# Attention outputs in a PSUM bank of the projections instead of one of the scores: a two-layer decoder trunk on one core

## The chip, the cores and the metric

The kernel runs on one core of a Trainium2 chip. The metric is the device time of one execution in microseconds (us). The engines are TensorE (PE in the profile, with PEld for its weight loads), VectorE (DVE), ScalarE (ACT), GpSimd (POOL) and SyncE (SP), which issues the DMAs. TensorE writes its results to PSUM, which this kernel uses as eight banks of 128 x 512 f32; the other engines read them from there.

## What is computed

```python
h = x
for l in range(2):
    h = h + hybrid_mixer(rmsnorm(h, attn_norm[l]), ...)
    h = h + memory_cross_attention(rmsnorm(h, cross_norm[l]), rmsnorm(mem, mem_norm[l]), ...)
    h = h + squared_relu_mlp(rmsnorm(h, mlp_norm[l]), w1[l], w2[l])
return rmsnorm(h, final_norm)
```

`h` is 512 tokens by 1024. The mixer has 16 causal attention heads with values 64 wide: six MLA heads, six differential heads (two softmaxes each, subtracted) and four MoBA heads. Their outputs are concatenated and go through one 1024 x 1024 output projection. Cross attention has four heads over 256 memory tokens. All is f32.

## The kernel before

Activations lie transposed, features on partitions and the 512 tokens on the free axis. An f32 product is made of three matmuls (`mm3`): each operand is held as a high part and a rest, and the product of the two rests is left out. A projection of 128 features is so 8 blocks x 3 = 24 matmuls 128 x 512, all in one PSUM bank (`proj_steps`, and `proj` for a whole one at once).

PSUM is shared out by tags. `psum(tag)` (L130 to L132) hands out a bank of its tag, `self.pbufs` says how many banks a tag has ("mm" 3, "s" 3, "t" 2), and `self.ptags` says which tag stands for another. Within a tag the banks are given out in the order of the program: a new tile takes the bank that comes free first, and its first matmul waits until that bank was read. What takes them:

- "mm": projections, and a few other products of the fillers.
- "s": the scores of one block of 128 queries (`scores`, L633). VectorE's pass L638 reads a score with its bias, and with that its bank is free; ScalarE's exponential (L640) works on a copy in SBUF.
- "o": the attention output of one head (`mix`, L668 to L680): eight matmuls of values with probabilities. ScalarE copies one half (L679) and VectorE adds the other half to it (L680); then the bank is free. The cross attention's outputs (`tail` in `cross_units`) take "o" too. Before, "o" stands for "s".
- "t": transposes of probabilities (L280), 128 x 128 each, which ScalarE (L660) and VectorE (L663) read.

In a mixer the 16 heads are run in eight pairs. A head is four units, one for each block of queries, with scores 128, 256, 384 and 512 wide: `start` makes scores, exponential and the division by their sum (L699 and L700; L700 of the 256-wide ones on GpSimd), `finish` makes the transposes, and after the fourth the head's `mix` follows. `pipeline` writes these one behind the other with a skew of two units between a start and its finish, and two more before the mix, and puts pieces of coming projections between them (`Filler`). When all heads are started the fillers are used up; `output` then writes the eight output projections, each over the heads' pairs in the order 3, 0, 4, 1, 5, 2, 6, 7, and their sums go to `h` in L1080.

The matmuls of `mm3` and of `scores` are not held to the order of the program: a scheduler of the compiler's places them where their inputs and their bank are there. So the first output projections can stand between the last attention steps, as far as they have a bank.

Of the kernel before, what the change touches and what calls it, by code (L numbers as in the profile page):

```python
# [49 lines left out]
class Filler:  # L50
# [17 lines left out]
    def run(self, time):  # L68

        busy = False  # L70
        while self.todo and self.todo[0][2] in self.over and time > 0:
            time -= self.step()
            busy = True
        return busy
# [27 lines left out]
class Trunk:  # L102
# [1313 lines left out]
    def run(self):  # L1416
        nc = self.nc
        self.bufs = {"A": 8, "B": 21, "tmp": 11, "small": 40, "raw": 4, "w": 5, "pt": 2}
        self.pbufs = {"mm": 3, "s": 3, "t": 2}
        self.ptags = {"o": "s"}  # L1420

        self.fill_order = "kv cq tok m0 d0 m1 d1 o0 m2 d2 o1 mem cross"
        self.unit_order = "m0 d0 m1 d1 o0 m2 d2 o1"
        self.fill_time = {1: 1870, 2: 1700}
        self.cross_fill_time = 4000
        self.mem_time = 300

        self.skew, self.tail_skew = 2, 2

        self.wait_n, self.wait_l, self.wait_d = 8, 3, 3  # L1430
        self.pow_d = 3
        self.chain_n, self.chain_l, self.chain_d, self.chain_k = 6, 12, 4, 2

        self.pool_kinds = ("mq", "kr", "q", "cq", "lat")
        self.vector_full = self.vector_all = False

        self.look, self.mlp_look = 2, 6
        self.plan = self.planned()
        self.blocks = sum(1 for _ in self.planned())
        self.fetched = 2  # L1440
        self.setup()
        g = self.gains
        self.sum_squares_start()
        self.hn = [self.norm_input(k, g["g_attn"][:, :KT], squares=False) for k in range(KT)]
        for k in range(KT):
            self.after(2 + k, lambda k=k: self.sum_squares_add(self.h[k], True))
        self.hnorm = Later()
        self.after(10, lambda: self.norm_of(self.hnorm, self.sq, NQ, 2))
        self.setup_gains()
        self.after(12, self.setup_rotary)  # L1450
        for n, part in enumerate(self.setup_distances()):
            self.after(24 + 2 * n, part)
        self.after(58, self.setup_lambda)
        self.memory_norm(34, 8)
        for l in range(L):
            gs = slice(l * KT, (l + 1) * KT)
            self.vector_full = True
            outs = self.mixer(l)
            self.vector_full = False
            self.output(self.a["w_out"][l], outs, g["g_cross"][:, gs], (3, 0, 4, 1, 5, 2, 6, 7))  # L1460
            outs = self.cross(l)
            parts = {n: [] for n in ("11", "21", "22", "t1", "t2", "t3", "t4", "y")}
            self.vector_all = True
            self.output(self.a["w_co"][l], outs, g["g_mlp"][:, gs], halves=parts)
            self.mlp(l, g["g_attn"][:, (l + 1) * KT:(l + 2) * KT] if l + 1 < L else None, parts)
            self.vector_all, self.look = False, 2
# [101 lines left out]
```

## Time and profile before

| | us |
|---|---|
| three runs | 1529.02, 1529.40, 1532.49 |
| median | 1529.40 |
| profiled execution, its own time | 1527.16 |
| its span in the trace | 1525.3 |

The profiled execution is the one that all rows below come from; its mean granted TensorE clock was 0.994. A span is the time from the first to the last instruction that the trace shows; the 1.86 us to the execution's own time lie around it. In a timeline a row gives the start of a group of like instructions, how long the group took, the engine, the line of the kernel, the operation, the tile that it writes and those it reads, shapes, the number of instructions, and in brackets the idle time of the engine just before it with what ended it.

### The profile page before, as it was taken

The page shows a single profiled execution, that of the slowest core. Times are in us where ns is not written, and L with a number is a line of the kernel's source. Part 1 is how long each engine was busy: PE and PEld are TensorE (multiplying, and loading weights), DVE is VectorE, ACT ScalarE, POOL GpSimd, SP SyncE. Part 2 cuts the span into 40 slices and gives each one's busy share as a digit, 9 for nine tenths or more (in the row PEclk, how much of TensorE's full clock was granted, in tenths as well). Part 3 has the DMA queues.
Part 4 walks back from the last instruction along what each step waited for, and adds up shares of the span by engine and source line. Part 5 has one row for each costly group of instructions (what it writes and reads, how often), then busy time and mean ns, then how long its engine had stood idle before and what let it go on. Part 6 is the DMA issues. An engine that isn't in the chain of part 4 may idle for free.

```text
span 1525.3 us, 24601 instructions
## 1 busy us (share of the span) xinstructions
PE 1481.2 (97%) x8648; PEld 1295.4 (85%) x8648; DVE 1060.3 (70%) x2422; ACT 856.9 (56%) x1887; POOL 365.3 (24%) x302
## 2 busy tenths in 40 slices
PE   7899999999999999999999999999999999999997
PEld 6778897888899899998897888878888989899887
DVE  7688888536699666675537898873378976677753
ACT  5666777535566544454446677764366654445441
POOL 2645375442000000000145446644400000000001
PEclk9999999999999999999999999999999999999998
DMA  4434543231223323322224535423212332333331
GB/s 153 127 106 138 153 132 111 77 96 49 87 74 125 111 88 105 100 96 98 96 77 112 150 113 154 118 86 95 98 34 76 106 123 90 104 96 106 111 97 55
DMA packets 90139, 157.24 MB, mean 103 GB/s; under 512 B 12065, under 2 KB 17057, under 8 KB 90017
## 3 DMA queue, kind: packets, MB, share of 16 engines
q1 hardware_dynamic: 89728, 155.63, 33.2%
q8 instruction: 68, 1.11, 0.3%
q14 instruction: 55, 0.44, 0.1%
q10 hardware_dynamic: 288, 0.05, 0.0%
HBM read 136.24 MB, written 2.10 MB: 91 GB/s over the span
## 4 chain that ended last, share of the span: by engine, by line
PE 71%; DVE 10%; issue 9%; ACT 4%; DMA 3%; POOL 2%; SPq 0%; POOLq 0%; DVEq 0%; ACTq 0%
PE mm L277 58%; PE s L277 10%; PE t L280 2%; DMA raw<-w 2%; DVE tmp L638 1%; ACT tmp L640 1%; DVE tmp L703 1%; POOL w L162 1%; DVE pt L663 1%; ACT B L140 1%; DMA raw<-w_in 1%; DVE small L1001 1%; POOL B L142 1%; PE t L277 1%; DVE tmp L261 1%
## 5 line engine op out<-in xcount | busy, mean ns | idle before, releaser
L277 PE MATMUL mm<-B,w 128*128 128x512 f32 (+1 forms) x2490 | 574.4, 386 | 1.3 <-POOL B L142 1.3
L277 PEld LDWEIGHTS mm<-B,w 128*128 128x128 f32 x2490 | 453.0, 189 | 95.1 <-POOL B L142 2.6
L277 PE MATMUL mm<-A,w 128*128 128x512 f32 (+1 forms) x1920 | 386.7, 351 | 6.2 <-ACT A L144 5.8
L157 ACT CAST w<-raw 128x512 fp32r<-128x512 f32 (+1 forms) x372 | 225.1, 607 | 269.6 <-PE mm L277 208.0
L277 PEld LDWEIGHTS mm<-A,w 128*128 128x128 f32 x1920 | 311.8, 190 | 50.7 <-ACT A L144 5.8
L162 POOL TENSOR_TENSOR w<-raw,w 128x512 fp32r<-128x512 f32 (+2 forms) x180 | 228.0, 1273 | 220.1 <-ACT w L157 177.9
L410 POOL TENSOR_TENSOR tmp<-tmp,tmp 128x512 f32<-128x512 f32 (+1 forms) x25 | 30.8, 1234 | 655.7 <-ACT tmp L407 653.6
L162 DVE TENSOR_TENSOR w<-raw,w 128x512 fp32r<-128x512 f32 x192 | 134.4, 700 | 35.5 <-ACT w L157 35.2
L640 ACT ACTIVATE tmp<-tmp,small 128x384 f32<-128x384 f32 (+3 forms) x176 | 99.0, 562 | 66.0 <-DVE small L638 63.2
L1080 DVE TENSOR_TENSOR h<-mm,h 128x512 f32<-128x512 f32 x92 | 63.3, 688 | 70.9 <-PE mm L277 70.6
L140 ACT CAST B<-tmp 128x512 fp32r<-128x512 f32 (+2 forms) x156 | 91.9, 591 | 24.1 <-DVE tmp L680 4.8
L277 PE MATMUL mm<-pt,B 128*128 128x256 f32 x768 | 102.9, 283 | 2.4 <-ACT tmp L1319 2.4
L277 PEld LDWEIGHTS mm<-pt,B 128*128 128x128 f32 x768 | 95.8, 189 | 3.4 <-ACT tmp L1319 3.4
L261 DVE TENSOR_TENSOR tmp<-raw,raw 128x512 f32<-128x512 f32 x64 | 44.0, 688 | 65.9 <-DMA raw<-w 65.9
L264 ACT CAST B<-tmp 128x512 fp32r<-128x512 f32 x96 | 59.5, 620 | 50.8 <-DVE tmp L261 50.8
L142 DVE TENSOR_TENSOR B<-tmp,B 128x512 fp32r<-128x512 f32 (+1 forms) x110 | 75.5, 686 | 12.3 <-ACT B L140 8.3
L280 PE MATMUL t<-ident,tmp 128*128 128x128 f32 (+1 forms) x444 | 74.5, 274 | 9.3 <-DVE tmp L828 3.3
L280 PEld LDWEIGHTS t<-ident,tmp 128*128 128x128 f32 (+1 forms) x444 | 54.2, 140 | 24.8 <-issue 4.2
L142 POOL TENSOR_TENSOR B<-tmp,B 128x512 fp32r<-128x512 f32 (+1 forms) x46 | 61.4, 1340 | 49.7 <-ACT B L140 47.4
L663 DVE TENSOR_TENSOR pt<-t,pt 128x256 fp32r<-128x256 f32 (+1 forms) x192 | 67.1, 370 | 6.3 <-ACT pt L660 5.4
L277 PE MATMUL s<-pt,B 128*128 128x512 f32 (+3 forms) x352 | 71.0, 345 | 0.0
L339 POOL TENSOR_TENSOR small<-small,mhalf 128x4 f32<-128x4 f32 (+2 forms) x19 | 23.4, 1229 | 198.2 <-DVE small L373 174.5
(195 smaller groups left out, 2135.8 us busy)
## 6 DMA issues: line engine op xcount, KB each, us to landing
raw<-w SPq DMA_DIRECT2D x256, 256.0 KB, 2.9
raw<-w_in SPq DMA_DIRECT2D x64, 256.0 KB, 3.0
st<-B SPq DMA_DIRECT2D x144, 64.0 KB, 2.0
raw<-w_ck SPq DMA_DIRECT2D x32, 256.0 KB, 2.9
raw<-w_cv SPq DMA_DIRECT2D x32, 256.0 KB, 2.7
raw<-w_out SPq DMA_DIRECT2D x32, 256.0 KB, 2.7
raw<-w_cq SPq DMA_DIRECT2D x32, 256.0 KB, 2.7
raw<-w_co SPq DMA_DIRECT2D x32, 256.0 KB, 2.6
```

Source lines behind the costliest of these rows:

```text
L140: nc.scalar.copy(hi, x)
L142: eng.tensor_tensor(lo, x, hi.bitcast(F32), ALU.subtract)
L157: self.nc.scalar.copy(w[:, 0, :], raw)
L162: eng.tensor_tensor(w[:, 1, :], raw, w[:, 0, :].bitcast(F32), ALU.subtract)
L261: nc.vector.tensor_tensor(got[name], x, y, op)
L264: nc.scalar.copy(w[:, 0, :], raw)
L277: self.in_order(self.nc.tensor.matmul(out, lhs, rhs, start=start, stop=stop, skip_group_check=open), hold)
L280: self.in_order(self.nc.tensor.transpose(out, x, self.ident))
L410: eng.tensor_tensor(s[:, :n], s[:, :n], self.sq[:, :n], ALU.add)
L640: nc.scalar.activation(t[:, :n], t[:, :n], AF.Exp, bias=st[:, 0:1], scale=-1.0, accum_out=st[:, 1:2])
L663: nc.vector.tensor_tensor(lo, src, hi.bitcast(F32), ALU.subtract)
L1080: nc.vector.tensor_tensor(self.h[m], ps, self.h[m], ALU.add)
```

## The change

One entry of a table: "o" stands for "mm". An attention output, in the mixers and in cross attention, takes one of the three banks of the projections, and the scores have their three banks with the few other tiles of "s" alone. The number of banks and all instructions stay as they are.

```diff
--- before.py
+++ after.py
@@ -1417,7 +1417,7 @@
         nc = self.nc
         self.bufs = {"A": 8, "B": 21, "tmp": 11, "small": 40, "raw": 4, "w": 5, "pt": 2}
         self.pbufs = {"mm": 3, "s": 3, "t": 2}
-        self.ptags = {"o": "s"}
+        self.ptags = {"o": "mm"}
 
         self.fill_order = "kv cq tok m0 d0 m1 d1 o0 m2 d2 o1 mem cross"
         self.unit_order = "m0 d0 m1 d1 o0 m2 d2 o1"
```

What this does to the order of instructions is seen in three places.

The first is TensorE's order near the end of layer 0's mixer. `s_` are the scores of the last head, `t_` transposes, `mm_3659`, `mm_3700` and `mm_3742` the first three output projections; `s_3599` is the output of the last head but one, `mm_3599` after the change. Before, and then after:

```order
L280 MATMUL t_3547<-ident,tmp_3473 128x128 x4
L277 MATMUL mm_3659<-B_1806,w_3459 128x512 x3
L277 MATMUL s_3556<-st_2331,st_2252 128x384
L277 MATMUL s_3556<-st_2332,st_2252 128x384
L277 MATMUL mm_3659<-B_1278,w_3459 128x512
L277 MATMUL s_3583<-st_2331,st_2252 128x512
L277 MATMUL s_3583<-st_2332,st_2252 128x512
L277 MATMUL t_3566<-halves,tmp_3511 128x2 x4
L277 MATMUL mm_3659<-B_1278,w_3459 128x512 x2
L277 MATMUL mm_3659<-B_2542,w_3485 128x512 x3
L277 MATMUL mm_3659<-B_2028,w_3459 128x512
L280 MATMUL t_3579<-ident,tmp_3516 128x128
```

```order
L280 MATMUL t_3547<-ident,tmp_3473 128x128 x4
L277 MATMUL s_3556<-st_2331,st_2252 128x384
L277 MATMUL s_3556<-st_2332,st_2252 128x384
L277 MATMUL s_3583<-st_2331,st_2252 128x512
L277 MATMUL s_3583<-st_2332,st_2252 128x512
L277 MATMUL t_3566<-halves,tmp_3511 128x2 x4
L280 MATMUL t_3579<-ident,tmp_3516 128x128
L280 MATMUL t_3593<-ident,tmp_3540 128x128 x2
L277 MATMUL mm_3599<-pt_3465,B_2550 128x512 x2
```

Between these transposes and scores stood ten matmuls of the projection `mm_3659` ahead of `t_3579`; now none does, and the last two scores stand one behind the other.

The second is the very end of the same mixer, with the last head's output (`s_3644`, then `mm_3644`). Before, and then after:

```order
L280 MATMUL t_3626<-ident,tmp_3586 128x128 x4
L277 MATMUL mm_3700<-B_2028,w_3662 128x512 x2
L277 MATMUL mm_3742<-B_1806,w_3703 128x512 x2
L280 MATMUL t_3635<-ident,tmp_3616 128x128 x4
L277 MATMUL s_3644<-pt_3578,B_2550 128x512 x2
L277 MATMUL s_3644<-pt_3578,B_2550 128x384 x2
L277 MATMUL s_3644<-pt_3578,B_2550 128x256 x2
L277 MATMUL s_3644<-pt_3578,B_2550 128x128 x2
L277 MATMUL mm_3742<-B_1806,w_3703 128x512
L277 MATMUL mm_3659<-B_3641,w_3485 128x512
```

```order
L280 MATMUL t_3626<-ident,tmp_3586 128x128 x4
L280 MATMUL t_3635<-ident,tmp_3616 128x128 x4
L277 MATMUL mm_3644<-pt_3578,B_2550 128x512
L277 MATMUL mm_3659<-B_1806,w_3459 128x512
L277 MATMUL mm_3644<-pt_3578,B_2550 128x512
L277 MATMUL mm_3644<-pt_3578,B_2550 128x384 x2
L277 MATMUL mm_3644<-pt_3578,B_2550 128x256 x2
L277 MATMUL mm_3644<-pt_3578,B_2550 128x128 x2
L277 MATMUL mm_3659<-B_1806,w_3459 128x512 x2
L277 MATMUL mm_3659<-B_1278,w_3459 128x512 x3
```

Before, 26 matmuls of output projections stand ahead of the last matmul of `s_3644`, from `mm_3659` to the third one's beginning. After, one matmul of `mm_3659` stands there, and the other 25 come behind. Layer 1 shows the same.

The third is the beginning of a differential pair in the middle of the mixer, with the waits that TensorE's instructions carry in brackets. The head's output `s_1826` (`mm_1826` after the change) stands right ahead of it. Before, and then after:

```order
L277 MATMUL s_1838<-st_1309,st_1194 128x128 [waits DMAHW5_49,DMAHW7_49,DMAHW3_49,DMAHW1_49]
L277 MATMUL s_1844<-st_1309,st_1194 128x128 [waits DMAHW4_49,DMAHW2_49,DMAHW6_49,DMAHW0_49,DVE_49]
L277 MATMUL mm_1769<-A_138,w_1652 128x512 x3
L277 MATMUL mm_1769<-A_141,w_1652 128x512 x3
L277 MATMUL mm_1769<-A_144,w_1652 128x512 x3
L280 MATMUL t_1865<-ident,tmp_1754 128x128 [waits DVE_49]
L280 MATMUL t_1865<-ident,tmp_1754 128x128 x2
L277 MATMUL s_1873<-st_1309,st_1194 128x256 [waits DVE_49]
L277 MATMUL s_1879<-st_1309,st_1194 128x256 [waits DVE_49]
L277 MATMUL mm_1897<-A_123,w_1772 128x512 x3
```

```order
L277 MATMUL s_1838<-st_1309,st_1194 128x128 [waits DMAHW5_49,DMAHW7_49,DMAHW3_49,DMAHW1_49]
L277 MATMUL s_1844<-st_1309,st_1194 128x128 [waits DMAHW4_49,DMAHW6_49,DMAHW2_49,DMAHW0_49]
L277 MATMUL mm_1769<-A_138,w_1652 128x512 x3
L277 MATMUL mm_1769<-A_141,w_1652 128x512 x3
L277 MATMUL mm_1769<-A_144,w_1652 128x512 x3
L280 MATMUL t_1865<-ident,tmp_1754 128x128 [waits DVE_49]
L280 MATMUL t_1865<-ident,tmp_1754 128x128 x2
L277 MATMUL s_1873<-st_1309,st_1194 128x256
L277 MATMUL s_1879<-st_1309,st_1194 128x256 [waits DVE_49]
L277 MATMUL mm_1897<-A_123,w_1772 128x512 x3
```

The second 128-wide score and the first 256-wide one lose their wait for VectorE; the second 256-wide one keeps it.

## Rows read from the trace of the kernel before

**Rows 1.** The page's head: span, busy time and number of instructions by engine.

```profile
span 1525.3 us, 24601 instructions
...
PE 1481.2 (97%) x8648; PEld 1295.4 (85%) x8648; DVE 1060.3 (70%) x2422; ACT 856.9 (56%) x1887; POOL 365.3 (24%) x302
```

**Rows 2.** PE's list of waits: waiting group, releaser: us in all, times, longest.

```profile
PE s L277 <- DVE small L638: 4.1, 6, 1.2
PE s L277 <- DVE tmp L680: 3.4, 7, 0.7
```

**Rows 3.** Timeline of PE at three scores that wait in layer 0's mixer.

```profile
100.52 0.33 PE L277 MATMUL s<-st,st 96*128 96x128 f32 x1 [1.09 <-DVE small L638]
...
109.05 0.51 PE L277 MATMUL s<-st,st 96*128 96x512 f32 x1 [0.19 <-DVE small L638]
...
144.51 0.59 PE L277 MATMUL s<-st,st 96*128 96x256 f32 x2 [0.47 <-DVE tmp L680]
```

**Rows 4.** Timeline of DVE around the last of them.

```profile
143.79 0.67 DVE L680 TENSOR_TENSOR tmp<-s,tmp 64x512 f32<-64x512 f32 x1
144.39 0.27 DVE L638 CUSTOM_DVE_ANT_0 tmp<-s,dneg 128x128 f32<-128x128 f32 x1
```

**Rows 5.** Timeline of PE at the end of both mixers, layer 0 first.

```profile
263.00 0.61 PE L277 MATMUL s<-st,st 128*128 128x384 f32 x2 [0.63 <-DVE tmp L680]
...
266.54 1.18 PE L277 MATMUL mm<-B,w 128*128 128x512 f32 x4
267.61 0.41 PE L280 MATMUL t<-ident,tmp 128*128 128x128 f32 x2
...
269.37 2.09 PE L277 MATMUL mm<-B,w 128*128 128x512 f32 x8
271.47 0.63 PE L280 MATMUL t<-ident,tmp 128*128 128x128 f32 x4
...
272.86 0.60 PE L280 MATMUL t<-ident,tmp 128*128 128x128 f32 x4
273.21 1.48 PE L277 MATMUL s<-pt,B 128*128 128x512 f32 x8
274.53 38.56 PE L277 MATMUL mm<-B,w 128*128 128x512 f32 x166
...
1007.91 0.62 PE L277 MATMUL s<-st,st 128*128 128x384 f32 x2 [0.62 <-DVE tmp L680]
...
1019.45 38.56 PE L277 MATMUL mm<-B,w 128*128 128x512 f32 x166
```

**Rows 6.** Timeline of DVE and PE at a projection's bank.

```profile
127.42 0.69 DVE L960 TENSOR_TENSOR tmp<-mm,rows 128x512 f32<-128x512 f32 x1
...
130.09 1.07 PE L277 MATMUL mm<-B,w 128*128 128x512 f32 x4
```

**Rows 7.** Timeline of POOL and DVE at the end of layer 0's mixer.

```profile
265.59 0.93 POOL L700 TENSOR_SCALAR tmp<-tmp,small 128x256 f32<-128x256 f32 x1 [6.57 <-DVE small L699]
...
268.88 0.68 DVE L638 CUSTOM_DVE_ANT_0 tmp<-s,dneg 128x512 f32<-128x512 f32 x1
...
270.84 0.48 DVE L700 TENSOR_SCALAR tmp<-tmp,small 128x512 f32<-128x512 f32 x1
```

**Rows 8.** Two gaps of PE; stretches: us, busy us by engine, granted clock, DMA.

```profile
76.40 0.63 PE L280 MATMUL t<-ident,tmp 128*128 128x128 f32 x4 [2.38 <-DVE tmp L700]
...
246.09 0.73 PE L277 MATMUL mm<-w,A 128*128 128x512 f32 x2 [1.11 <-DVE B L145]
...
76.00:80.00 4.00, 3.60 (x13) 3.15 (x14) 3.83 (x13) 2.52 (x8) 1.01 (x1) 0.64 0.29 69
80.00:84.00 4.00, 4.00 (x18) 3.20 (x18) 2.63 (x9) 2.06 (x6) 1.30 (x2) 0.94 0.38 87
244.00:248.00 4.00, 2.89 (x14) 2.05 (x13) 3.58 (x11) 2.39 (x7) 1.82 (x2) 1.00 0.38 92
```

## The prediction

> **What bounds the kernel now.** I read the page's head first: TensorE (PE) is busy 97% of the 1525.3 us span, VectorE (DVE) 70%, ScalarE (ACT) 56% [rows 1]. The time is therefore PE's work plus the few places where PE stands still, and the change can act in two ways only: it takes PE waits away or makes new ones, and it changes what PE has to fill a wait with. So I read PE's list of waits next. Scores wait for VectorE's L638 (the pass that frees a score's bank) six times, 4.1 us together, and for L680 (the add that frees the bank of an attention output) seven times, 3.4 us [rows 2]: at most 7.5 us, 0.5% of the span. Then I read the timeline at those waits, to see what would be late next, and the order of instructions against the changed one, to see what moves. The largest move is at the end of each mixer, so the rest of my reading is the timeline of that stretch, 263 to 274.5 us in layer 0. Layer 1 repeats it: from its wait of 0.62 us at 1007.91 to the start of the long run of projections at 1019.45 are 11.54 us, against 11.53 in layer 0 [rows 5].
>
> **Bulk: the score waits.** With "o" out of the scores' banks, scores alone rotate over the three. In the order a score loses its wait for VectorE and the next one keeps it. The trace says what that is worth. At 144.51 a score stood 0.47 us for L680 [rows 3]. L680 ran from 143.79 for 0.67 us, and right behind it, from 144.39 for 0.27 us, stands the L638 that frees the next bank [rows 4]. Without L680 the first score of the pair goes some 0.45 us earlier, but the second needs the bank of that L638, which ends at 144.66, while it now starts about 0.3 us behind the first, at 144.8. The gain is 0.1 us. The other kind, 1.09 us at 100.52, ends earlier too, but a 512-wide score at 109.05 already waits 0.19 us for L638 [rows 3]: what PE gains it gives back there, since VectorE is no faster. I take 0.1 us for each of six or so such places: **-0.6 us**. The bounds are 0 and the whole of what stands in rows 2 less the 0.63 and 0.62 us of the two mixer ends [rows 5], 7.5 - 1.25 = 6.2 us.
>
> The Trainium skill, in "Perfetto Trace Analysis", section "Optimization Strategy", says that the same gap repeating on the engine that should be saturated can mean that there isn't enough PSUM for the next tile to be allocated. By that page the whole 6.2 us would come back here; it is a rival below. The trace agrees that a bank is waited for, and does not agree that a bank is all that is missing.
>
> **Bulk: the projections.** An "o" now takes one of the projections' three banks, and the order shows new waits at the start of some projections. One is the projection at 130.09, which takes the bank that L960 reads from 127.42 for 0.69 us [rows 6]: it is free 1.98 us before it is wanted. I cost these waits at nothing. What covers them is those 2 us; if VectorE were later by more, each would cost the difference.
>
> **The mixer's end.** In the order before, 26 matmuls of the first three output projections stand between the last attention steps of a layer; they fill PE while VectorE and ScalarE finish the softmax. A projection there needs a bank of "mm". After the change the last two outputs stand ahead of the projections in that pool, and of the 26 only one stands before the last output's end; 25 come behind it. One dense matmul costs 38.56 / 166 = 0.232 us [rows 5], so **25 x 0.232 = 5.8 us** of PE work goes from inside the waits to behind them.
>
> Against that the chain of the last attention steps, now alone on PE, gets shorter. By rows: the 384-wide score goes at 261.43 or so instead of 263.00, since its wait of 0.63 us was for L680 [rows 5]; that is worth little, as VectorE reads the scores one after another. The first transposes were ready before PE had time for them: POOL's L700 ended at 265.59 + 0.93 = 266.52 [rows 7], and its transposes began at 267.61 behind projections [rows 5]. So they begin at 266.6, a gain of 1.0 us. From there the chain belongs to VectorE and ScalarE: the 512-wide L638 began at 268.88 behind short passes, its L700 at 270.84 [rows 7], and the four transposes at 271.47 [rows 5], 0.15 us after L700's end at 271.32. Moving each step up as far as its inputs allow, I get transposes at 271.1, the next four at 272.05 (were 272.86), the last output from 272.4 (was 273.21). The chain shortens by **0.8 us**. So the long run of projections, which began at 274.53, begins at 273.7 and has 25 matmuls more: 5.8 - 0.8 = **+5.0 us a layer, +10.0 us** for two. Bounds: +5.8 a layer if the chain does not shorten at all; and 0 if every step up to the last output moves up by as much as the fillers took from it (a rival).
>
> **The clock.** After the change PE stands idle about 1.5, 1.4, 2.5 and 0.4 us within 8 us there; the long one lies between the transposes of the 384-wide and those of the 512-wide score. What a gap does to PE's clock I take from the rows nearest in length. After 2.38 us at 76.40 the granted clock was 0.64 of 2.4 GHz in 76 to 80 us and 0.94 in 80 to 84; after 1.11 us at 246.09 it stayed 1.00 [rows 8]. 0.64 is a mean of the two levels, 1.2 and 2.4 GHz. The loss is (0.36 + 0.06) x 4 = 1.7 us of work at full clock. 2.5 us is nearest to the 2.38, so I count one such loss per layer, at 1.5 us because part of it falls into the gaps: **+3.0 us**; bounds 0 and 3.4.
>
> The skill's page "TensorE: Matmul & The Clock Gate", section "A second HAM failure mode: psum-queue depth-cycling", tells of a kernel in which PE idles briefly between groups as it cycles through PSUM banks, and its clock goes back and forth between the two levels. By that rule the removed waits of the bulk would have cost clock as well, and taking them away would gain more than their length. The row at 246.09 does not agree for gaps of about 1 us; the row at 76.40 agrees for 2.4.
>
> **Sum**: -0.6 + 10.0 + 3.0 = +12.4 us on the profiled execution's 1527.16 us: 1539.6. The median of the runs, 1529.4, is 2.24 above that execution, so the forecast is **1541.8 us**, 0.8% slower. A measurement can tell about 0.3% here, 4.6 us.
>
> **Rivals.**
> - *No clock loss.* The gaps are broken up by transposes and the short output matmuls, so the clock stays at 1.00 as at 246.09. 1541.8 - 3.0 = 1538.8 us. Chance 0.25; forecast as it stands 0.46.
> - *The banks were all that scores waited for* (the page's rule). A third score ahead lets VectorE run without its own waits, and the whole 6.2 us come back instead of 0.6: 1541.8 - 5.6 = 1536.2 us, or 1533.2 without the clock loss. Against it stands L638 right behind L680 [rows 4]. Chance 0.18; a third of it within 0.3%.
> - *Faster: the fillers held the chain up.* If PE's projections delayed each of the late steps, as they did the one at 267.61, the chain shortens by the full 5.8 us, the end costs nothing, and the bulk waits come back: 1529.4 - 6.2 = 1523.2 us. It decides from a shortening of 5.8 us a layer on. Against it: the steps at 271.47 and 272.86 began within 0.3 us of their inputs. Chance 0.06.
> - *Two clock losses a layer*, one in the middle and one at the end: 1541.8 + 3.4 = 1545.2 us. Chance 0.05.
>
> **How the numbers follow.** Forecast, no-clock case, clock-twice case and two thirds of the bank case are slower by over 0.3% (above 1534.0): 0.46 + 0.25 + 0.05 + 0.12 = 0.88, less some 0.06 for a chain that shortens by half of the 5.8: 0.82. Same takes 0.06 + 0.06 = 0.12, faster 0.06. The forecast's own range is 1539 to 1544; the range for 8 in 10 goes down to the bank case without clock loss, 1533, and up to 1545.
>
> **What would show it.** In the changed profile: a gap of about 2.5 us on PE before the transposes near 271 us, waiting for L700; one matmul run of about 190 from 273.7 us on; granted clock below 0.9 in one slice between 270 and 278 us and again some 745 us later; waits for L680 gone from PE's list and those for L638 not shorter by more than a us or two. The forecast is wrong if the run of projections begins before 270 us, if fillers still stand between the last steps, or if scores no longer wait for VectorE at all.

## The result, and the profile after

The changed kernel takes 1549.58 us (median of six runs, 1543.39 to 1554.16), the kernel before 1529.07 (six runs, 1524.74 to 1532.49): 20.5 us more, a ratio of 1.0136 with a 95% interval of 1.0108 to 1.0164. Slower was forecast, but at 1541.8 us with a range up to 1545.0; the time lies above it. The profiled execution took 1554.16 us with a span of 1552.4, 27.1 us longer than the one of before.

The page's head and PE's list of waits of the changed kernel (columns as in [rows 1, 2]):

```profile
span 1552.4 us, 24600 instructions
...
PE 1493.0 (96%) x8648; PEld 1307.1 (84%) x8648; DVE 1062.7 (68%) x2422; ACT 858.7 (55%) x1887; POOL 362.9 (23%) x302
```

```profile
PE s L277 <- DVE small L638: 13.2, 12, 2.1
...
PE t L280 <- DVE small L699: 4.9, 2, 2.9
PE t L280 <- DVE small L344: 4.6, 2, 2.3
```

Three things are to be seen. PE does the same 8648 instructions and is 11.8 us longer busy with them: a lower clock, not more work. The waits of scores for L680 (3.4 us before) are gone, and those for L638 have grown from 4.1 us to 13.2, by more than went; 3.3 us of the 13.2 are one wait at each mixer end. And there are new waits of transposes: those for L344 (the row names a small pass beside the L700 that they need) are the late gaps at the two mixer ends, those for L699 two gaps in the middle.

PE's timeline at the end of layer 0's mixer, after the change:

```profile
262.51 1.48 PE L277 MATMUL mm<-pt,B 128*128 128x512 f32 x8
...
265.42 0.59 PE L277 MATMUL s<-st,st 128*128 128x384 f32 x2
267.65 0.73 PE L277 MATMUL s<-st,st 128*128 128x512 f32 x2 [1.64 <-DVE small L638]
...
270.60 0.66 PE L280 MATMUL t<-ident,tmp 128*128 128x128 f32 x2 [0.83 <-POOL tmp L700]
270.92 2.59 PE L277 MATMUL mm<-pt,B 128*128 128x512 f32 x8
273.30 0.86 PE L280 MATMUL t<-ident,tmp 128*128 128x128 f32 x3
276.44 2.10 PE L280 MATMUL t<-ident,tmp 128*128 128x128 f32 x8 [2.27 <-DVE small L344]
278.18 0.78 PE L277 MATMUL mm<-pt,B 128*128 128x512 f32 x1
...
324.10 1.79 PE L277 MATMUL mm<-A,w 128*128 128x512 f32 x7
```

It is [rows 5] without its fillers. The gaps are where the prediction had put them: 1.64, 0.83 and 2.27 us. But the eight matmuls of an attention output, 1.48 us long for the third last at 262.51, take 2.59 us for the last but one at 270.92. The granted clock of the same stretch says why (stretch, busy time by engine, PEclk, DMA share, GB/s), after the change and then before:

```profile
268.00:272.00 4.00, 3.01 (x16) 2.45 (x15) 3.05 (x15) 1.97 (x8) 0.92 (x1) 0.66 0.04 15
272.00:276.00 4.00, 2.16 (x10) 1.76 (x8) 2.17 (x9) 1.82 (x5) 1.67 (x1) 0.50 0.00 0
276.00:280.00 4.00, 3.56 (x14) 3.06 (x15) 2.63 (x9) 0.97 (x3) 0.00 (x0) 0.56 0.00 0
```

```profile
266.00:270.00 4.00, 4.00 (x24) 3.27 (x24) 2.10 (x10) 1.95 (x6) 1.46 (x2) 1.00 0.00 0
270.00:274.00 4.00, 3.99 (x23) 3.10 (x22) 3.69 (x13) 1.78 (x6) 0.72 (x1) 1.00 0.00 0
```

0.50 is the lower level, 1.2 of 2.4 GHz. At the end of layer 0 it held for (0.34 + 0.50 + 0.44) x 4 / 0.5 = 10.2 us, three times the (0.36 + 0.06) x 4 / 0.5 = 3.4 us that [rows 8] had shown after the gap at 76.40. It fell in the stretch that follows the gap of 1.64 us, ahead of the long gap on which the forecast had hung it.

The low clock also held up the last steps. ScalarE's exponential of the last, 512-wide score (L640) stands in its queue behind its copy of the last output but one (L679), and the copy waits for PE. Before, and then after the change:

```profile
269.29 0.58 ACT L679 COPY tmp<-s 64x512 f32<-64x512 f32 x1 [0.86 <-PE s L277]
269.78 0.72 ACT L640 ACTIVATE tmp<-tmp,small 128x512 f32<-128x512 f32 x1
```

```profile
273.54 0.58 ACT L679 COPY tmp<-mm 64x512 f32<-64x512 f32 x1 [1.87 <-PE mm L277]
...
274.47 0.72 ACT L640 ACTIVATE tmp<-tmp,small 128x512 f32<-128x512 f32 x1
```

The copy starts as soon as PE's eight matmuls end (269.25 before, 273.51 after). What PE loses in them to the clock, 1.1 us, stands in the chain of the last steps.

I call "the end" the time from the start of the third last attention output to the first matmul of the cross attention's queries, behind all eight output projections. It holds the same useful work in all kernels here. After the change it is 324.10 - 262.51 = 61.6 us in layer 0 and 62.1 in layer 1. Before, its bounds in layer 0 were these, 54.6 us apart, and 54.6 in layer 1:

```profile
258.30 0.48 PE L277 MATMUL s<-pt,B 128*128 128x512 f32 x1
...
312.92 5.63 PE L277 MATMUL mm<-A,w 128*128 128x512 f32 x24
```

So 14.4 us of the 27 were in the two ends of the profiled execution. When the two traces are laid side by side matmul by matmul, 10.5 us more went elsewhere, nearly all of it in the middle of the mixers, and 2.1 us in the first 80 us, whose instructions the change does not touch. How much of the middle is the change and how much is one execution, a profile cannot tell; that was the first question.

### The profile page after: what moved, and what is told of

Its sections match the earlier page's. It is cut to its first block, busy times and chain, and to the rows that moved or that the text cites. A ratio compares the mean times of both kernels' runs of the same rounds, so it can differ in the third digit from the quotient of the medians.

```text
span 1552.4 us, 24600 instructions
## 1 busy us (share of the span) xinstructions
PE 1493.0 (96%) x8648; PEld 1307.1 (84%) x8648; DVE 1062.7 (68%) x2422; ACT 858.7 (55%) x1887; POOL 362.9 (23%) x302
## 3 DMA queue, kind: packets, MB, share of 16 engines
q8 instruction: 68, 1.11, 0.3%
## 4 chain that ended last, share of the span: by engine, by line
PE 70%; DVE 11%; issue 9%; ACT 5%; DMA 3%; POOL 2%; SPq 0%; POOLq 0%; DVEq 0%; ACTq 0%
PE mm L277 60%; PE s L277 7%; PE t L280 2%; DVE tmp L638 2%; DMA raw<-w 2%; ACT tmp L640 1%; DVE pt L663 1%; DVE tmp L703 1%; POOL B L142 1%; DVE small L1001 1%; DVE B L142 1%; POOL w L162 1%; ACT B L140 1%; PE t L277 1%; DVE tmp L700 1%
## 5 line engine op out<-in xcount | busy, mean ns | idle before, releaser
L277 PE MATMUL mm<-pt,B 128*128 128x256 f32 (+3 forms) x1120 | 178.8, 307 | 3.0 <-ACT tmp L1319 3.0
L277 PEld LDWEIGHTS mm<-pt,B 128*128 128x128 f32 x1120 | 158.2, 193 | 11.2 <-ACT tmp L1319 4.2
L640 ACT ACTIVATE tmp<-tmp,small 128x384 f32<-128x384 f32 (+3 forms) x176 | 98.9, 562 | 66.7 <-DVE small L638 65.0
L280 PE MATMUL t<-ident,tmp 128*128 128x128 f32 (+1 forms) x444 | 79.1, 287 | 18.4 <-DVE small L699 4.9
L142 POOL TENSOR_TENSOR B<-tmp,B 128x512 fp32r<-128x512 f32 (+1 forms) x46 | 61.6, 1345 | 49.5 <-ACT B L140 44.3
L663 DVE TENSOR_TENSOR pt<-t,pt 128x256 fp32r<-128x256 f32 (+1 forms) x192 | 66.9, 370 | 5.9 <-ACT pt L660 5.0
L277 PE MATMUL mm<-w,A 128*128 128x512 f32 (+1 forms) x288 | 67.2, 372 | 2.3 <-DVE B L145 1.6
```

The source lines that it names most:

```text
L142: eng.tensor_tensor(lo, x, hi.bitcast(F32), ALU.subtract)
L277: self.in_order(self.nc.tensor.matmul(out, lhs, rhs, start=start, stop=stop, skip_group_check=open), hold)
L280: self.in_order(self.nc.tensor.transpose(out, x, self.ident))
L640: nc.scalar.activation(t[:, :n], t[:, :n], AF.Exp, bias=st[:, 0:1], scale=-1.0, accum_out=st[:, 1:2])
L663: nc.vector.tensor_tensor(lo, src, hi.bitcast(F32), ALU.subtract)
```

## The experiments

The theories, as they stood before the first runs. **A**: two parts by themselves, the ends (lost cover and the clock) and the middle (waits that moved to the next score, and the clock). **B**: only the ends cost anything, the middle's loss is scatter; for the kernel with useless matmuls, B names another rival, that gaps alone cost and the clock does not. **C**: the scores did lack the bank. **D**: at the ends it is a wait for a bank, not the lost cover. **E** came later: three banks are too few for projections and outputs together. Ratios are to the kernel before, measured beside each; the ends are read from one profiled execution of each kernel.

| kernel | median us | ratio, 95% interval | ends, layer 0 and 1, us |
|---|---|---|---|
| before | 1528 to 1529 | | 54.6, 54.6 |
| changed | 1549.58 | 1.0136, 1.0108 to 1.0164 | 61.6, 62.1 |
| last two outputs in "s" | 1531.95 | 1.0023, 1.0011 to 1.0034 | 54.4, 54.4 |
| only these two in "mm" | 1548.08 | 1.0134, 1.0118 to 1.0149 | 63.1, 64.0 |
| only cross attention's in "mm" | 1528.70 | 1.0003, 0.9993 to 1.0014 | 54.6, 54.6 |
| before, three projections held | 1545.35 | 1.0111, 1.0096 to 1.0125 | 63.0, 63.0 |
| changed, 25 useless matmuls an end | 1541.95 | 1.0085, 1.0069 to 1.0102 | 59.8, 59.8 |
| before, two projections held | 1540.19 | 1.0078, 1.0060 to 1.0095 | 59.6, 59.7 |
| last but one only in "mm" | 1536.87 | 1.0052, 1.0038 to 1.0065 | 59.6, 59.3 |
| changed, projections written early | 1535.57 | 1.0043, 1.0027 to 1.0058 | 56.5, 56.5 |
| before, projections written early | 1530.00 | 1.0010, 1.0000 to 1.0020 | 55.4, 55.4 |
| mm 4, s 2, outputs in "mm" | 1555.48 | 1.0171, 1.0154 to 1.0188 | 63.1, 63.0 |
| outputs in a bank of their own, s 2 | 1538.33 | 1.0059, 1.0047 to 1.0072 | 54.3, 54.3 |
| outputs in "t" | 1536.34 | 1.0047, 1.0031 to 1.0064 | 54.3, 54.2 |
| ninth and last two in "s", rest "mm" | 1530.45 | 1.0013, 1.0002 to 1.0024 | 54.4, 54.4 |
| ninth only in "mm" | 1531.72 | 1.0010, 1.0001 to 1.0019 | 54.6, 54.6 |

### Where it is: the ends or the middle

`mixes` counts the calls of `mix`, 16 a layer. Of each edit the deciding lines are shown; where outputs are told apart, cross attention's `tail` names its tag itself. The last two outputs of a mixer back in the scores' banks, all others and cross attention in those of the projections:

```diff
-        ps = self.psum("o")
+        ps = self.psum("s" if self.mixes % 16 >= 14 else "mm")
+        self.mixes += 1
```

> The last two attention outputs of each mixer take a bank of the scores again, all others (28 of 32, and those of cross attention) one of the projections. Theory A, two parts: the mixers' ends cost what the timelines show there (6.3 and 7.4 us, together 13.7), and the middle of the mixers costs the rest by itself (3.0 and 7.5 us, 10.5 in the profiled run), since the wait that was taken from one score stands at the next one, longer, and lowers the clock. By it this kernel stays 5 to 11 us above the kernel before (1534 to 1540 us), the waits of scores for L638 stay above 8 us, and the ends have their fillers and a clock of 1.00. Theory B, the middle's loss is scatter of one profiled run (late weights, passes of VectorE that happened to collide with GpSimd) and only the ends cost anything: within 0.3% of the kernel before, 1525 to 1533 us. Theory C, the bank is what the scores lacked: 1521 to 1525 us, faster than before.

1531.95 us. The ends are as short as before. What the other 28 outputs and cross attention cost is 0.23%, 1531.95 - 1528.16 (before, in these runs) = 3.8 us: less than theory A's 5 to 11 us, inside B's range, and not nothing. Theory C falls: with three banks for the scores alone the kernel is not faster.

The reverse, only the last two in the projections' banks (`"mm" if self.mixes % 16 >= 14 else "s"`, cross attention in "s"):

> Only the last two attention outputs of each mixer take a bank of the projections; all others, and those of cross attention, take one of the scores as before. Theory A: the ends alone, 13 to 14 us above the kernel before (1542 to 1543 us), with gaps of PE of some 2.3 us before the 512-wide transposes and a low clock there. Theory B: the ends are the whole of the loss, 18 to 21 us (1547 to 1550). My forecast's terms for the ends were 10.0 + 3.0 us (1542).

1548.08 us, 19.9 more than before, all but the whole of the change's 20.5. Theory B's number; A's 13 to 14 us is too small. Cross attention alone (`self.psum("mm")` in its `tail`, `"s"` in `mix`):

> Only the outputs of cross attention take a bank of the projections; the mixers are as before. All theories: the timelines show 0.5 us a layer there, so 0 to 1.2 us in all, not to be told from the kernel before (1525 to 1533 us). If it is slower by 4 us or more, a part of the loss lies in cross attention that the alignment of the two traces did not show.

No difference that can be told. So of the change's 20.5 us four outputs of 32 make nearly all.

### Lost cover or a wait for the bank

The kernel before, with its banks, but fillers held back: `in_order` ties a held matmul behind the one written before it.

```diff
-        mm(out, lhs[0], rhs[0], start=first, stop=False, hold=False, open=open)
+        mm(out, lhs[0], rhs[0], start=first, stop=False, hold=self.held, open=open)
...
+            self.held = halves is None and i < 3
             ps = self.proj(w[m], lambda k: (outs[k][:, 0, :], outs[k][:, 1, :]), S, order)
+            self.held = False
```

> The kernel before, all outputs in the banks of the scores, but the matmuls of the first three output projections of each mixer are held to the order of the program, so that none can stand between the last attention steps: the fillers are gone without a change of banks. If the ends cost what they do because the fillers are gone (theory A), it is slower by about as much as the kernel in which only the last two outputs change banks, 12 to 14 us (1541 to 1543 us), with the same gap of 2.3 us and low clock at the ends. If it is the bank itself (a wait of the last outputs for a bank, theory D), it is within 3 us of the kernel before.

1545.35 us and ends of 63.0 us, without a single bank changed; the loss of 17.2 us is more than the 12 to 14 expected, and nothing like D's 3. Theory D falls: the cover is what is lost.

### What the lost cover costs: moved work or the clock

In the changed kernel, 12 and 13 matmuls that compute nothing of use stand where the fillers stood, each in the bank of the output that overwrites it:

```diff
         ps = self.psum("o")
+        for j in range({14: 12, 15: 13}.get(self.mixes % 16, 0)):
+            self.mm(ps, self.outs[3][:, 0, :P], self.outs[3][:, 0, :], True, True, hold=False)
+        self.mixes += 1
```

> The changed kernel, with 12 and 13 additional matmuls 128 x 512 that compute nothing of use, written into the bank of the last but one and of the last attention output of each mixer before that output begins; they stand where the 25 output projections stood before. The work that moved behind the ends stays there. Theory A (clock): of some 18 to 20 us at the ends about 9 are the low clock that follows the gaps. With the gaps filled the granted clock stays at 1.00 there, and what is left is 25 x 0.232 = 5.8 us a layer, 11.6 in all, with the 3.5 us that the 28 other outputs cost: 1528.2 + 15.1 = 1543 us (1541.5 to 1545), 5 to 8 us faster than the changed kernel although it does 50 matmuls more. Theory B (gaps alone, the clock costs nothing of weight): useless work cannot help; as slow as the changed kernel or slower, 1549 to 1554 us.

1541.95 us: 50 matmuls more, and 7.6 us faster than the changed kernel. PE's timeline and the granted clock of this kernel, end of layer 0:

```profile
268.90 2.75 PE L277 MATMUL mm<-B 128*128 128x512 f32 x11
271.69 0.63 PE L280 MATMUL t<-ident,tmp 128*128 128x128 f32 x4
```

```profile
264.00:268.00 4.00, 4.00 (x24) 3.24 (x23) 2.29 (x13) 1.60 (x7) 0.93 (x1) 1.00 0.06 23
268.00:272.00 4.00, 3.96 (x24) 3.20 (x23) 3.74 (x16) 2.21 (x6) 1.67 (x1) 1.00 0.00 0
272.00:276.00 4.00, 4.00 (x24) 3.27 (x23) 2.70 (x7) 1.85 (x4) 0.00 (x0) 1.00 0.00 0
```

The eleven useless matmuls fill the gap ahead of the four transposes, the clock stays at 1.00, and the ends are 59.8 us, 5.2 longer than before. That is the moved work by itself: 25 x 0.232 = 5.8 us less 0.6. What the useless matmuls gave back, 7.6 us by the medians, is the clock's part. Its size is known only roughly. The intervals of the two ratios allow some 3 to 13 us. In the profiled executions the ends of the changed kernel cost 14.4 us, 4.0 more than these 10.4; those of the kernels that lost the same fillers in another way cost 16.8 (three projections held) and 17.8 (only the last two outputs in "mm"), 6.4 and 7.4 more.

Which gap lowers it? Two kernels with half the fillers each. The kernel before with `0 < i < 3` in place of `i < 3` above keeps the 12 early fillers and has the late gap:

> The kernel before, with only the second and the third output projection held to the order of the program: 12 of the 26 fillers stay, all ahead of the 512-wide transposes' gap, 14 go behind the end. If the low clock begins with the first gaps of the end (the 1.64 us before the last score, in the changed kernel), these 12 keep the clock up until the late gap, and the low stretch shrinks from 10 us to about 3.4: (14 x 0.232 - 0.5 + 1.5) = 4.2 us a layer, 1528.2 + 8.5 = 1536.7 us (1535 to 1539). If it hangs on the late gap of 2.3 us alone, the whole clock loss of 4.7 us a layer stays: 1528.2 + 2 x (2.7 + 4.7) = 1543 us. If the loss is in proportion to the fillers taken away: 14/25 of 17.2 = 9.6, 1537.8 us, with a low stretch as long as when all are held.

1540.19 us, between the first and the second number; the low stretch is the 3.4 us of the first, as the rows below show. And `"mm" if self.mixes % 16 == 14 else "s"`, which keeps the late fillers and has the early gaps:

> Only the last output but one of each mixer takes a bank of the projections. In the order the 14 fillers ahead of it are gone (PE has its early gaps, of up to 1.6 us), but 12 or 13 stand behind it again, in the late gap of 2.3 us. It is the counterpart of the kernel that held the second and third projection, which kept the early fillers, had the late gap and one low stretch of 3.4 us a layer, and cost 11.0 us. If the long low stretch of the changed kernel (10 us) begins with the early gaps, the clock is low here for 3.4 to 6.8 us a layer, and gone by the late steps: 13 x 0.232 = 3.0 us moved + 1.5 to 3 of clock, 1528.5 + 9 to 12 = 1538 to 1541 us. If only the late gap lowers the clock, 1.00 throughout: 1528.5 + 5 = 1533.5 us.

1536.87 us, a little under the first number. Its early gaps in layer 0 are 0.42, 1.33 and 0.83 us. The granted clock at layer 0's end, with the two projections held, and then with the last output but one in "mm":

```profile
272.00:276.00 4.00, 2.00 (x13) 1.70 (x13) 3.01 (x13) 2.39 (x8) 1.67 (x1) 1.00 0.00 0
276.00:280.00 4.00, 3.42 (x13) 2.79 (x14) 2.80 (x10) 0.81 (x3) 0.00 (x0) 0.57 0.00 0
```

```profile
264.00:268.00 4.00, 3.13 (x15) 2.73 (x15) 2.89 (x16) 2.01 (x8) 0.92 (x1) 0.59 0.14 52
268.00:272.00 4.00, 4.00 (x16) 3.62 (x16) 2.11 (x7) 1.90 (x5) 1.67 (x1) 0.56 0.00 0
272.00:276.00 4.00, 4.00 (x24) 3.18 (x22) 2.91 (x12) 0.95 (x5) 0.00 (x0) 1.00 0.00 0
```

With the late gap alone PE was at the low level for 0.43 x 4 / 0.5 = 3.4 us; with the early gaps alone for (0.41 + 0.44) x 4 / 0.5 = 6.8 us. Layer 1 of both kernels shows the same. So early and late gaps both lower the clock, and in layer 0 of the changed kernel the 10.2 us look like the two, one behind the other. But this is no fixed price of a gap. In layer 1 of the changed kernel, gaps of 1.64, 0.15, 0.93 and 2.32 us, nearly those of layer 0, were followed by only (0.20 + 0.23 + 0.34 + 0.08) x 4 / 0.5 = 6.8 us at the low level:

```profile
1028.00:1032.00 4.00, 2.92 (x16) 2.41 (x15) 3.07 (x15) 2.10 (x8) 0.92 (x1) 0.80 0.08 29
1032.00:1036.00 4.00, 2.07 (x10) 1.77 (x8) 2.23 (x9) 1.82 (x5) 1.67 (x1) 0.77 0.00 0
1036.00:1040.00 4.00, 3.23 (x13) 2.76 (x14) 2.73 (x10) 1.26 (x3) 0.00 (x0) 0.66 0.00 0
1040.00:1044.00 4.00, 4.00 (x20) 3.45 (x19) 2.04 (x3) 1.20 (x2) 0.00 (x0) 0.92 0.00 0
```

With only the last two outputs in "mm" it was 13.7 us in layer 1 (granted clock 0.62, 0.50, 0.50 and 0.67 in 1020 to 1036 us) after 10.2 in layer 0. What decides how long the clock stays low after such gaps these runs do not show.

### Why the fillers went: number of banks or order

> The changed kernel (all outputs take a bank of the projections), but four blocks (12 matmuls) of the first output projection are written in the program ahead of the last output but one, and four of the second ahead of the last output. Number of banks and their sharing are those of the changed kernel. In the order 24 fillers stand ahead of the end of the last output again. Theory A (what the ends lost is the cover, and it was lost since tiles of one tag get their banks in the order of their first writes in the program): the ends cost nothing or 1 us a layer, and what is left is the 3.5 us of the other outputs: 1529 to 1535 us, 15 to 20 us faster than the changed kernel, clock 1.00 at the ends. Theory E (three banks are too few for projections and outputs together): 1540 us or more, with waits of PE for L680 or L1080 at the ends.

The first blocks of two projections are written ahead of the last two outputs, and the rest of them where they were:

```diff
+        if self.mixes % 16 >= 14:
+            g = self.early_proj(self.mixes % 16 - 14)
+            self.early.append(g)
...
+            for _ in range(4):
+                next(g)
...
         ps = self.psum("o")
```

1535.57 us, 14 us faster than the changed kernel with the same three banks, and the clock at the ends at 1.00. The ends are 1.9 us longer than before, where 1 was expected at most: the program's early blocks also brought other steps forward, and PE has two new gaps, of 0.72 and 0.51 us, which end with VectorE's passes L1032 and L1040 for the last differential pair. Theory E falls; it falls again with four banks, `{"mm": 4, "s": 2, "t": 2}`:

> Outputs in the projections' banks, with four banks for these and two for the scores. In the order the ends are as in the changed kernel: one filler ahead of the last output's end. Theory A: a bank more does not help, the ends cost 18 to 20 us, and the scores wait longer with two banks: 1550 to 1562 us. Theory E (too few banks there): the ends cost nothing, and only the scores' waits count, as in the kernel with a bank of its own for the outputs: 1535 to 1542 us.

1555.48 us, ends no shorter than with three. So it is the order. In the order of this kernel still a single filler stands ahead of the last output's end. Tiles of a tag get their banks in the order in which the program takes and first writes them, with four as with three; the output projections are written behind the last outputs.

The same early blocks in the kernel before bring nothing:

> The kernel before (outputs in banks of the scores) with the same two projections begun early in the program. In the order 30 fillers instead of 26 stand ahead of the end of the last output. If PE still has idle time there that they can fill, 4 x 0.232 = 0.9 us a layer, 1.9 us faster than before: 1526 to 1528 us, which a measurement can hardly tell from no change; if the fillers hold the chain up, 1529 to 1533 us.

1530.00 us, level within what can be told: the fillers were already enough.

### Is there a better place for the outputs

> Attention outputs get a bank of their own: projections 3, scores 2, outputs 1, transposes 2. The order keeps 26 fillers at the ends, as before. If outputs may not stand in the projections' queue and nothing else is wrong with taking them from the scores, the ends cost nothing; the scores pay for their third bank with waits for L638 (the wait of 4.1 us grows). Theory A: 1530 to 1540 us by longer waits of scores. If the third bank of the scores was of no use: within 0.3% of before, 1525 to 1533.

1538.33 us (`{"mm": 3, "s": 2, "o": 1, "t": 2}`, no tag standing for another). The ends are whole, and the scores pay for their third bank, in PE's list of waits (L638, 4.1 us before):

```profile
PE s L277 <- DVE small L638: 13.0, 24, 1.5
```

> Attention outputs take one of the two banks of the transposes; scores and projections keep three each. The order keeps 25 to 30 fillers at the ends. The next transposes wait while an output stands in a bank until L680 (some 2 us), so waits of transposes for L680 of 0.5 to 2 us each should show, 32 outputs: 1535 to 1560 us. If the projections between the units cover them and the scores' waits for L680 vanish (3.4 us), it is faster than before: 1522 to 1526 us.

1536.34 us (`{"o": "t"}`). Here the waits of scores for L638 shrink to 1.5 us and those for L680 are gone, the ends are as short as before, and it is still 0.5% slower; the list of waits has new ones in the tag "t" instead, outputs for L663 first:

```profile
PE t L277 <- DVE pt L663: 4.7, 6, 1.5
...
PE t L277 <- DVE small L699: 2.5, 2, 1.4
```

L663 reads transposes, so it frees their bank and also makes the probabilities that the output needs; which of the two was waited for the row does not tell. No kernel tried was faster than the one before.

### The middle's 3.8 us

Beside the waits of scores the order has one more place where fillers moved: ahead of the first output of a MoBA pair, the ninth of 16. PE's order there, before and after:

```
L277 MATMUL mm_2492<-A_2486,w_2418 128x256 x6
L277 MATMUL mm_2592<-A_2465,w_2495 128x256 x3
L280 MATMUL t_2556<-ident,tmp_2409 128x128 x2
L277 MATMUL s_2562<-pt_2305,B_1719 128x512 x2
```

```
L277 MATMUL mm_2492<-A_2486,w_2418 128x256 x3
L277 MATMUL s_2574<-B_697,B_1711 128x128 x3
L280 MATMUL t_2556<-ident,tmp_2409 128x128 x2
L277 MATMUL mm_2562<-pt_2305,B_1719 128x512 x2
```

Six short matmuls of the memory projections went behind the output, as at the ends. The gap at this place in layer 1: before, after, and with the last two outputs in "s":

```profile
937.80 0.44 PE L280 MATMUL t<-ident,tmp 128*128 128x128 f32 x2 [0.42 <-DVE tmp L1030]
```

```profile
955.06 0.42 PE L280 MATMUL t<-ident,tmp 128*128 128x128 f32 x2 [2.86 <-DVE small L699]
```

```profile
940.98 0.41 PE L280 MATMUL t<-ident,tmp 128*128 128x128 f32 x2 [2.46 <-DVE small L700]
```

Scores in the middle are the other candidate. Two places of PE's timeline after the change:

```profile
146.68 0.39 PE L277 MATMUL s<-st,st 96*128 96x256 f32 x1 [0.53 <-DVE small L638]
...
240.41 0.38 PE L277 MATMUL s<-st,st 96*128 96x256 f32 x1 [1.89 <-DVE small L638]
```

The first is the pair of scores whose first one stood 0.47 us for L680 in [rows 3]; now the second stands 0.53 us for L638. At the second place, waits of 0.92 us at 233.65 and 0.24 us at 236.67 before became a single one of 1.89. Two kernels take the candidates apart: `"s" if self.mixes % 16 in (8, 14, 15) else "mm"`, and the ninth alone, `"mm" if self.mixes % 16 == 8 else "s"`.

> As the kernel with the last two outputs of a mixer in banks of the scores and all others in those of the projections (1.0023), but the ninth output, the first of a MoBA pair, is in a bank of the scores too. In the order the six short fillers stand ahead of it again, as in the kernel before. If the middle's loss is this lost cover: the gaps at 195 and 940 us are back at 0.4 to 1.4 us, no low clock there, and the kernel is level with the one before, ratio 0.9985 to 1.0010. If it is the scores' waits, which stay as they are in this kernel (some 9 us for L638): ratio 1.0015 to 1.003.

> The kernel before, with the ninth output of each mixer alone in a bank of the projections. The scores' waits stay as in the kernel before (L638 4.1 us, L680 3 us or so). If the middle's loss is the lost cover there: gaps of 1.5 to 2.5 us at 195 and 938 us, a low clock behind the second, ratio 1.0015 to 1.003. If it is the scores' waits: 0.999 to 1.001.

Ratios of 1.0013 (1.0002 to 1.0024) and 1.0010 (1.0001 to 1.0019). The first lies between its two hypotheses, the second at the upper end of that of the scores' waits. By the medians each candidate has about half of the 0.23%, but the intervals allow any other split, so this is not shown. The traces say a little more. With the ninth output alone in "mm" the fillers were gone, but the gaps were 1.09 us in layer 0 and 1.08 in layer 1, shorter than expected, and the clock stayed up:

```profile
942.18 0.41 PE L280 MATMUL t<-ident,tmp 128*128 128x128 f32 x2 [1.08 <-DVE small L700]
...
942.00:946.00 4.00, 3.82 (x30) 3.77 (x31) 3.96 (x8) 2.49 (x5) 2.85 (x3) 1.00 0.58 186
```

With the ninth and the last two in "s" the fillers were back ahead of the output, and the gap was still 1.72 us in both layers, with the clock at 1.00 in layer 0 and at 0.77 in 938 to 942 us in layer 1. So the lost fillers are not all of that gap either. That stays open.

## Why the prediction was wrong

*What bounds the kernel; where the change acts.* Right: PE's work, its gaps, and what fills them. The order read for the ends was right in every row. Of the gaps, 1.5, 1.4, 2.5 and 0.4 us were forecast; measured were 1.64, then 0.16 and 0.83 in place of the 1.4, then 2.27, and no fourth in layer 0.

*Moved work, +10.0 us.* Right in size: with the clock kept up by useless matmuls the ends were 5.2 us longer each, 10.4. The shortening of the chain by 0.8 us, a part of that term, did not come in the changed kernel itself: from the third last to the last output were 273.21 - 258.30 = 14.9 us before and 278.18 - 262.51 = 15.7 after. "From there the chain belongs to VectorE and ScalarE" left out that ScalarE's exponential stands behind a copy that waits for PE's output, and PE made that output at the low clock, in 2.59 instead of 1.48 us.

*The clock, +3.0 us with an upper bound of 3.4: this is the step that failed.* It measured 7.6 us by the medians (1549.58 - 1541.95), and 4.0 to 7.4 at the ends of the profiled executions. The ends together, forecast at 13.0 us, cost 19.9 when they alone were changed. I had counted one low stretch of 3.4 us a layer and hung it on the longest gap, at the price of the nearest single gap. The runs show that the early gaps lower the clock as well: 10.2 us at the low level in layer 0 and 6.8 in layer 1. The row that spoke against this, 1.11 us at 246.09 with the clock at 1.00 [rows 8], was one gap in busy surroundings; the ends have three within 11 us. The rival "two clock losses a layer" had the right kind, at 1545.2 us and a chance of 0.05; it should have been the forecast. The rival "no clock loss" got 0.25 and was wrong outright.

*The bulk, -0.6 us: wrong in sign, the second step that failed.* It is +3.8 by the medians. That the waits come back at the next score was right; that each would come back a little shorter was not. They came back longer. With all outputs but the last two in "mm", scores wait 8.9 us for L638, 1.4 of them at the ends; outside the ends that is 7.5 us where 4.1 + 3.4 less 1.25, 6.2 us, stood before. That the bulk could at worst cost nothing stood on no row. PE's list of waits of that kernel:

```profile
PE s L277 <- DVE small L638: 8.9, 11, 1.9
```

And the lost fillers at the ninth output, which the order showed, were not in the sum at all.

*The projections' new waits, nothing.* Right as far as seen: no wait of a projection for its bank is among the first rows of PE's list.

The terms as measured, 10.4 + 7.6 + 3.8 = 21.8 us, and the 20.5 of the whole agree within the scatter of the medians. The range ended at 1545 because the clock had been bounded from one row and the bulk had not been allowed to cost anything.

*The rules that were cited.* The Trainium skill, "Perfetto Trace Analysis", section "Optimization Strategy", says that a repeated gap can mean a lack of PSUM. As the sole cause this fell here: with three banks for themselves the scores waited longer, for VectorE. The Trainium skill, "TensorE: Matmul & The Clock Gate", section "A second HAM failure mode: psum-queue depth-cycling", says that PE's short idling between groups costs throughput through the clock. The ends show this, with gaps of 0.8 to 2.3 us. For the bulk, where I had set it aside by one row, the runs point both ways: the kernel with the ninth and the last two outputs in "s" has a gap of 1.72 us with the clock at 0.77 in layer 1, and one of 1.72 us with the clock at 1.00 in layer 0.

## What to carry to other kernels

In this kernel work that filled an engine's gaps was lost when its buffer queued behind what it was to cover. Before a tag is shared, look in the order for what is written ahead of the fillers in that tag, and where a new tile must go there, write the first blocks of the fillers ahead of it. Price lost cover on TensorE twice, as moved work and as clock, and for the clock count all the gaps that stand close together, not the longest alone. Ask also which engine waits for the work that the low clock slows. To tell the two prices apart, put useless matmuls into the gaps.

## What was not expected of the hardware

Fifty matmuls that compute nothing made the changed kernel 7.6 us faster (1549.58 to 1541.95 us), as the granted clock at the ends stayed at 1.00 instead of 0.50 to 0.66. And the length of a gap did not tell what the clock would do: nearly the same four gaps were followed by 10.2 us at the low level in layer 0 and by 6.8 in layer 1 of one execution.
